# The last two up tiles of layer 0 by token halves, the context halves between the two halves of the last down product

## The chip, the cores and the metric

The kernel runs on one core of one Trainium2 chip. The metric is the device time of one execution in microseconds (us), the median of several runs; lower is better. Engine names are the profile's: PE multiplies matrices, DVE and POOL are the vector engines, ACT is the scalar engine, SP issues the transfers.

## The reference

A trunk of two layers works on 256 latent tokens and 256 context tokens of width 1024, in float32. Each layer is a token mixer of four branches and then a gated convolutional feed-forward network (FFN). Cut to the FFN and what follows it:

```python
def conv_ffn(h, w_up, conv_w, conv_b, w_down):          # D_FF = 2816
    a, g = jnp.split(h @ w_up, 2, axis=-1)
    return (jax.nn.silu(dwconv(a, conv_w, conv_b)) * g) @ w_down   # conv of 3 tokens

x = x + mod[:, 5] * rmsnorm(conv_ffn(h, ffn_up[l], ...), norm_g[l, 3])
...
h = rmsnorm(x, norm_g[l, 0]) * (1.0 + mod[:, 1]) + mod[:, 0]       # the next layer's input
```

Context tokens pass through layer 0 with the same weights and a modulation of their own; in layer 1 only the latent tokens go through the FFN, but both kinds are read by the mixer.

## The kernel before, in words

Activations lie with channels on the partitions and the 512 tokens along the free axis, latents in columns 0 to 255, context in 256 to 511. Each float32 product is made of three products of reduced-precision (`fp32r`) parts: `hi*hi`, `hi*lo`, `lo*hi` (`mm3`, lines 135 to 137), where `lo` is the value less its rounded `hi`. A weight tile of 128x1024 takes this way: SP loads it into one of 4 buffers `raw`, ACT rounds it into `hi` (L122), and DVE (one instruction) or POOL (four of 256 columns) subtracts to make `lo` (L131). `wload` deals the tiles out: `turn[1]` is the share of POOL, 0.6 in the FFN of layer 0 and 0.8 from its last down product on. There are 4 buffers of `hi` and 4 of `lo`, so the cast of a tile waits until PE is done with the tile loaded four before.

Layer 0's FFN has 22 tiles of 128 hidden channels. `up(i, ...)` multiplies tile i's two weight tiles with the normed input `h2` into two PSUM banks, `ua` (to be convolved) and `ug` (the gate); then ACT scales `ua` (L1482), DVE adds the two neighbours (L1486, L1488, after which the bank is free), ACT applies silu (L1490), DVE multiplies by `ug` (L1491), ACT rounds to `fh` (L1492) and POOL subtracts to `fl` (L1493). `ua`, `ug` and the down product's `o` share a PSUM pool (`mm`) of 3 banks. The hidden channels are taken in three segments, tiles 0 to 5, 6 to 13 and 14 to 21; after each, `out_gemm` multiplies the segment with the down weights and adds into `y`. The last segment's down product runs by token halves, 8 output tiles m for the latents, then 8 for the context; the second half goes through m backwards, and the weights of m = 4 to 7 are kept in their buffers from the first half (`keep`=4), so that 12 weight tiles are loaded for the 16 products.

After a half of the last segment, `chain` follows for it: a sum of squares over the output channels (PE row sums `st`, L170; DVE `rs_v`, L176; POOL `rs_y`, L151; PE spreads it into `R`, L182), the scaled addition into `x` channel tile by channel tile (DVE L341; POOL or DVE L343; ACT squares, L279; DVE adds them, L285), a second `st`, `rs_v`, `rs_y`, `R`, and the next layer's input `hn` (DVE L300, ACT L301, DVE L302). `chain` is a generator; `pump()` advances it one step, and `gemm_p` calls `pump` in the middle and at the end of each product of 24 matmuls. So its steps stand between matmuls by count: the latents' chain is pumped through the context's down product, the context's chain through the first products of layer 1 (Fourier `f`, then `u`). Tile's scheduler may move an instruction a little; each engine then executes its own queue in order. `hn` lies in the same buffers as `h2`.

## Time and profile before

| | us |
|---|---|
| median of 3 runs | 1406.83 (1405.43 to 1408.57) |
| the profiled execution, whole | 1407.98 |
| its span in the trace | 1406.2 |
| PE busy in the span | 1336.9 (95%) |
| DVE, ACT, POOL busy | 863.8, 621.6, 849.7 |

The span is what the trace shows from the first to the last instruction; the execution's own time lies 1.8 us above it. All starts below are counted from the span's start. Layer 0 ends and layer 1 begins at about 908 us.

### The profile page before, as it was taken

The page shows a single profiled execution, that of the slowest core. Times are in us where ns is not written, and L with a number is a line of the kernel's source. Part 1 is how long each engine was busy: PE and PEld are TensorE (multiplying, and loading weights), DVE is VectorE, ACT ScalarE, POOL GpSimd, SP SyncE. Part 2 cuts the span into 40 slices and gives each one's busy share as a digit, 9 for nine tenths or more (in the row PEclk, how much of TensorE's full clock was granted, in tenths as well). Part 3 has the DMA queues.
Part 4 walks back from the last instruction along what each step waited for, and adds up shares of the span by engine and source line. Part 5 has one row for each costly group of instructions (what it writes and reads, how often), then busy time and mean ns, then how long its engine had stood idle before and what let it go on. Part 6 is the DMA issues. An engine that isn't in the chain of part 4 may idle for free. (4 is left out here: it accounts for less than half of the span.)

```text
span 1406.2 us, 22765 instructions
## 1 busy us (share of the span) xinstructions
PE 1336.9 (95%) x8514; PEld 1195.1 (85%) x8514; DVE 863.8 (61%) x1554; ACT 621.6 (44%) x1098; POOL 849.7 (60%) x978
## 2 busy tenths in 40 slices
PE   8798999999999979999799999898999999899998
PEld 6597899888878979888688889897999998899997
DVE  4738766888777465599886553768847543532323
ACT  4435534444324445423231333466636545554443
POOL 1533234456764676567565546675556898689894
PEclk9999999999999999999899999999999999999999
DMA  9422223433443443466577443343324455355552
GB/s 347 137 77 81 69 105 106 135 120 140 160 162 107 147 151 114 138 227 211 195 253 270 155 160 106 116 135 104 108 76 135 147 164 184 123 184 200 183 181 75
DMA packets 61935, 210.55 MB, mean 150 GB/s; under 512 B 7145, under 2 KB 9729, under 8 KB 61569
## 3 DMA queue, kind: packets, MB, share of 16 engines
q1 hardware_dynamic: 61824, 209.10, 44.1%
q8 instruction: 67, 1.10, 0.3%
q14 instruction: 44, 0.35, 0.1%
HBM read 208.01 MB, written 1.06 MB: 149 GB/s over the span
## 5 line engine op out<-in xcount | busy, mean ns | idle before, releaser
L131 POOL TENSOR_TENSOR lo<-raw,hi 128x256 fp32r<-128x256 f32 x814 | 698.6, 890 | 392.2 <-ACT hi L122 373.9
L122 ACT CAST hi<-raw 128x1024 fp32r<-128x1024 f32 (+2 forms) x284 | 293.7, 1036 | 336.1 <-PE ua L136 76.6
L131 DVE TENSOR_TENSOR lo<-raw,hi 128x1024 fp32r<-128x1024 f32 (+2 forms) x79 | 122.3, 1548 | 89.6 <-ACT hi L122 89.5
L135 PE MATMUL gt<-hh,hi 128*128 128x512 f32 (+1 forms) x512 | 175.3, 342 | 1.0 <-DVE sig L782 1.0
L137 PE MATMUL gt<-hh,lo 128*128 128x512 f32 (+1 forms) x512 | 172.8, 338 | 0.6 <-POOL lo L131 0.6
L136 PE MATMUL gt<-hl,hi 128*128 128x512 f32 (+1 forms) x512 | 172.2, 336 | 0.0
L135 PE MATMUL ug<-hh,hi 128*128 128x256 f32 (+1 forms) x384 | 125.9, 328 | 10.4 <-DVE ca L1488 10.4
L232 DVE SCALAR_TENSOR_TENSOR ar<-ar,scb 128x1024 f32<-128x1024 f32 x80 | 122.4, 1534 | 15.6 <-DMA ar<-w_adaT 14.8
L136 PE MATMUL ug<-hl,hi 128*128 128x256 f32 (+1 forms) x384 | 125.5, 327 | 0.0
L135 PE MATMUL ua<-hh,hi 128*128 128x256 f32 (+1 forms) x384 | 124.3, 324 | 0.9 <-ACT hh L301 0.9
L137 PE MATMUL ug<-hh,lo 128*128 128x256 f32 (+1 forms) x384 | 125.1, 326 | 0.0
L136 PE MATMUL ua<-hl,hi 128*128 128x256 f32 (+1 forms) x384 | 124.0, 323 | 0.1
L137 PE MATMUL ua<-hh,lo 128*128 128x256 f32 (+1 forms) x384 | 123.8, 322 | 0.0
L137 PEld LDWEIGHTS gt<-hh,lo 128*128 128x128 f32 x512 | 96.6, 189 | 11.6 <-POOL lo L131 0.8
L135 PEld LDWEIGHTS gt<-hh,hi 128*128 128x128 f32 x512 | 96.7, 189 | 11.0 <-DVE sig L782 1.2
L136 PEld LDWEIGHTS gt<-hl,hi 128*128 128x128 f32 x512 | 96.8, 189 | 10.0
L135 PEld LDWEIGHTS ug<-hh,hi 128*128 128x128 f32 x384 | 74.2, 193 | 16.9 <-issue 8.5
L135 PE MATMUL o<-fh,hi 128*128 128x256 f32 (+1 forms) x240 | 81.0, 337 | 0.0
L136 PE MATMUL mm<-lo,hh 128*128 128x256 f32 x272 | 78.6, 289 | 2.4 <-DVE lo L131 2.4
L136 PE MATMUL o<-fl,hi 128*128 128x256 f32 (+1 forms) x240 | 80.5, 335 | 0.0
L137 PE MATMUL o<-fh,lo 128*128 128x256 f32 (+1 forms) x240 | 80.5, 335 | 0.0
L135 PEld LDWEIGHTS ua<-hh,hi 128*128 128x128 f32 x384 | 72.8, 190 | 7.6 <-ACT hh L301 1.1
(312 smaller groups left out, 3250.6 us busy)
## 6 DMA issues: line engine op xcount, KB each, us to landing
raw<-w_up SPq DMA_DIRECT2D x92, 512.0 KB, 4.0
ar<-w_adaT SPq DMA_DIRECT2D x80, 512.0 KB, 4.1
raw<-w_gate SPq DMA_DIRECT2D x64, 512.0 KB, 3.5
raw<-w_tm SPq DMA_DIRECT2D x24, 512.0 KB, 3.5
raw<-w_dr SPq DMA_DIRECT2D x22, 512.0 KB, 3.5
raw<-w_dn SPq DMA_DIRECT2D x20, 512.0 KB, 3.7
ada_w<-w_ada SPq DMA_DIRECT2D x16, 512.0 KB, 8.3
raw<-w_branch SPq DMA_DIRECT2D x16, 512.0 KB, 3.6
```

What stands on the lines that cost most here:

```text
L122: nc.scalar.copy(hi[:, :n], raw[:, :n])
L131: e.tensor_tensor(out=lo[:, s], in0=raw[:, s], in1=hi[:, s].bitcast(F32), op=ALU.subtract)
L135: nc.tensor.matmul(ps, a[0], b[0], start=start, stop=False)
L136: nc.tensor.matmul(ps, a[0], b[1], start=False, stop=False)
L137: return nc.tensor.matmul(ps, a[1], b[0], start=False, stop=stop)
L232: nc.vector.scalar_tensor_tensor(out=raw if st == ns - 1 else junk, in0=raw, scalar=0.5, in1=scb[:, st, :], op0=ALU.mult, op1=ALU.mult, ac ...
```

## The change

The up tiles 20 and 21 of layer 0 are computed by halves: before the last down product for the latents only, with their weights loaded, and again between the two halves of that product for the context, with the same four weight tiles loaded and split a second time. The last down product keeps no weights (`keep=0`), so its second half loads m = 0 to 7 again, in forward order. The output projection `w_out` still keeps four.

```diff
--- before.py
+++ after.py
@@ -1395,7 +1395,7 @@
                         nc.sync.dma_start(out=x[c0][k], in_=I["xT"][:, k, c0:c0 + 256])
             yn = None if last else YNorm(zap, TQ, "za")
 
-            def out_gemm(parts, act, src, yn, ks, w0=0, n=1024, add=False, stat=False, lag=0, nt=0):
+            def out_gemm(parts, act, src, yn, ks, w0=0, n=1024, add=False, stat=False, lag=0, nt=0, keep=CFG["keep"]):
                 kept = {}
                 late = []
                 for c0, c1 in parts:
@@ -1405,7 +1405,7 @@
                     for i, m in enumerate(ms):
 
                         wt = kept.pop(m, None) or wload(src(m), n)
-                        if c0 == 0 and len(parts) > 1 and m >= KD - CFG["keep"]:
+                        if c0 == 0 and len(parts) > 1 and m >= KD - keep:
                             kept[m] = wt
                         ps = mmb("o")
                         if c0 == 0 and i < lag:
@@ -1553,8 +1553,19 @@
                           nc.gpsimd if CFG["yp"] & 2 else None)
             yn = None if last else YNorm(zap, TQ, "za")
             for s, (a, b) in enumerate([] if last else SEGS):
-                ups(nu, min(b + 1, KF))
+                split = 2 if s == 2 else 0
+                ups(nu, min(b + 1, KF) - split)
                 nu = min(b + 1, KF)
+
+                def part_ups(c0, c1):
+                    for i in range(KF - split, KF):
+                        if c0 == 0:
+                            f[i] = new_f()
+                        w2 = [wload(I["w_up"][l, i, q]) for q in range(2)]
+                        up(i, w2[0], w2[1], c0, c1, f[i])
+
+                if split:
+                    part_ups(*parts[0])
                 nk = b - a
                 acts = [f[a + j] for j in range(nk)]
                 if s == 2:
@@ -1574,9 +1585,11 @@
                     if not last:
                         A1n = mod_scale(P[1]["vec"], mods[1], 1, 0, True)
                         hn.append(new_h())
-                    for c0, c1 in out_gemm(parts, acts, src, yn, range(nk), add=True, stat=True, lag=CFG["dl"]):
+                    for c0, c1 in out_gemm(parts, acts, src, yn, range(nk), add=True, stat=True, lag=CFG["dl"], keep=0):
                         pump(64)
                         pend.append(chain(yn, c0, c1, G2, hn[0], A1n, mods[1], 0, CFG["g3"][c0 > 0]))
+                        if c0 == 0:
+                            part_ups(*parts[1])
             tick(len(todo))
 
     es_ctx = ExitStack()
```

Three places of the instruction queues, with buffer numbers kept in the names. First POOL, at the end of the latents' down product, before: the first `rs_y` of the latents' chain stands behind the subtracts of the last down weights (`lo_8237` is m = 7).

```order
L131 TENSOR_TENSOR lo_8126<-raw_8123,hi_8125 128x256 x4
L131 TENSOR_TENSOR lo_8199<-raw_8196,hi_8198 128x256 x4
L131 TENSOR_TENSOR lo_8237<-raw_8234,hi_8236 128x256 x4
L151 TENSOR_TENSOR rs_y_8291<-rs_v_8289,mh_98 128x2
L131 TENSOR_TENSOR lo_8435<-raw_8432,hi_8434 128x256
L343 TENSOR_TENSOR x0_0_4494<-x0_0_4494,y0_5891 128x256
L131 TENSOR_TENSOR lo_8435<-raw_8432,hi_8434 128x256 x3
```

Behind it come the four context weights that this half has to load (`lo_8435` is the first).

POOL in the changed kernel at the same `rs_y`; `lo_8279`, `lo_8288` and `lo_8382` are weight tiles of the context's up halves (the fourth, `lo_8376`, is on DVE), `lo_8469` is the context's first down weight.

```order
L131 TENSOR_TENSOR lo_8237<-raw_8234,hi_8236 128x256 x4
L131 TENSOR_TENSOR lo_8279<-raw_8276,hi_8278 128x256 x4
L131 TENSOR_TENSOR lo_8288<-raw_8285,hi_8287 128x256 x4
L131 TENSOR_TENSOR lo_8382<-raw_8379,hi_8381 128x256 x4
L151 TENSOR_TENSOR rs_y_8310<-rs_v_8308,mh_98 128x2
L131 TENSOR_TENSOR lo_8469<-raw_8466,hi_8468 128x256
L343 TENSOR_TENSOR x0_0_4494<-x0_0_4494,y0_5891 128x256
L131 TENSOR_TENSOR lo_8469<-raw_8466,hi_8468 128x256 x3
```

The `rs_y` now stands behind the fourth up weight. Second, DVE in the changed kernel, in the latents' chain just before its second `st`; `ca_8458` is tile 21's context half.

```order
L343 TENSOR_TENSOR x0_5_4499<-x0_5_4499,y5_5896 128x256
L341 SCALAR_TENSOR_TENSOR y6_5897<-y6_5897,ms5_7955,R_8324 128x256
L341 SCALAR_TENSOR_TENSOR y7_5898<-y7_5898,ms5_7955,R_8324 128x256
L285 TENSOR_TENSOR sq_8329<-sq_8329,sq_8438 128x256
L1486 SCALAR_TENSOR_TENSOR ca_8458<-ua_8388,vec_100,ca_8458 128x255
L285 TENSOR_TENSOR sq_8329<-sq_8329,sq_8455 128x256
L1488 SCALAR_TENSOR_TENSOR ca_8458<-ua_8388,vec_100,ca_8458 128x255
L343 TENSOR_TENSOR x0_7_4501<-x0_7_4501,y7_5898 128x256
L131 TENSOR_TENSOR lo_8610<-raw_8607,hi_8609 128x1024
L1491 TENSOR_TENSOR ca_8458<-ca_8458,ug_8389 128x256
```

The additions that free the bank of `ua_8388` and the product with `ug_8389` now stand between the chain's additions of squares. PE's queue there, where `o_8475` and `o_8516` are the context's down products of m = 0 and 1, and `fh_7877` and `fl_7878` are tile 21:

```order
L135 MATMUL o_8516<-fh_7392,hi_8509 128x256
L136 MATMUL o_8516<-fl_7393,hi_8509 128x256
L135 MATMUL o_8475<-fh_7877,hi_8468 128x256
L137 MATMUL o_8516<-fh_7392,lo_8510 128x256
L135 MATMUL o_8516<-fh_7477,hi_8509 128x256
L136 MATMUL o_8475<-fl_7878,hi_8468 128x256
L137 MATMUL o_8475<-fh_7877,lo_8469 128x256
L136 MATMUL o_8516<-fl_7478,hi_8509 128x256
```

The second output tile is begun before the first ends, and the first waits for tile 21's context half. The second `st` of the latents' chain follows five rows below this; it and the second `R` have exactly as many matmuls behind the end of the latents' down product as before, 132 and 144. Third, POOL at the start of layer 1, before: the first `rs_y` of the context's chain, `lo_8904` the fifth weight tile of layer 1.

```order
L131 TENSOR_TENSOR lo_8663<-raw_8660,hi_8662 128x256 x4
L131 TENSOR_TENSOR lo_8807<-raw_8804,hi_8806 128x256 x4
L151 TENSOR_TENSOR rs_y_8683<-rs_v_8681,mh_98 128x2
L131 TENSOR_TENSOR lo_8904<-raw_8901,hi_8903 128x256 x4
L343 TENSOR_TENSOR x256_0_4513<-x256_0_4513,y0_5891 128x256
L343 TENSOR_TENSOR x256_2_4515<-x256_2_4515,y2_5893 128x256
L343 TENSOR_TENSOR x256_4_4517<-x256_4_4517,y4_5895 128x256
L131 TENSOR_TENSOR lo_8913<-raw_8910,hi_8912 128x256 x3
```

Ahead of this `rs_y` stand layer 1's second and third weight tiles.

And in the changed kernel, where `lo_8989` and `lo_9032` are layer 1's third and fourth weight tiles and `lo_9089` its fifth:

```order
L131 TENSOR_TENSOR lo_8845<-raw_8842,hi_8844 128x256 x4
L131 TENSOR_TENSOR lo_8989<-raw_8986,hi_8988 128x256 x4
L131 TENSOR_TENSOR lo_9032<-raw_9029,hi_9031 128x256 x4
L151 TENSOR_TENSOR rs_y_8865<-rs_v_8863,mh_98 128x2
L343 TENSOR_TENSOR x256_0_4513<-x256_0_4513,y0_5891 128x256
L131 TENSOR_TENSOR lo_9089<-raw_9086,hi_9088 128x256 x4
L343 TENSOR_TENSOR x256_2_4515<-x256_2_4515,y2_5893 128x256
L343 TENSOR_TENSOR x256_4_4517<-x256_4_4517,y4_5895 128x256
L343 TENSOR_TENSOR x256_6_4519<-x256_6_4519,y6_5897 128x256
```

The fourth tile was on DVE before and is on POOL now, ahead of `rs_y`; the fifth moved from ahead of `x256_0` to between `x256_0` and `x256_2`. On ACT the copy `ft` that the second Fourier product reads (L822) stood behind the square of `x256_0`, and stands behind that of `x256_2` now.

## Rows read from the trace of the kernel before

**Rows 1.** Timeline of PE, 842 to 920 us: start, duration, instruction, [idle before, releaser].

```profile
842.22 0.39 PE L135 MATMUL ua<-hh,hi 128*128 128x512 f32 x1
...
853.10 0.28 PE L135 MATMUL o<-fh,hi 128*128 128x256 f32 x1
...
875.50 0.50 PE L170 MATMUL st<-one,sq 128*128 128x1 f32 x4
...
879.20 0.61 PE L182 MATMUL R<-cst,rs_y 128*128 128x128 f32 x4
...
893.16 0.58 PE L170 MATMUL st<-one,sq 128*128 128x1 f32 x4 [0.75 <-DVE sq L285]
895.35 0.61 PE L170 MATMUL st<-one,sq 128*128 128x1 f32 x4 [1.61 <-ACT sq L279]
...
900.62 1.22 PE L182 MATMUL R<-cst,rs_y 128*128 128x128 f32 x4 [3.09 <-POOL rs_y L151]
...
908.37 0.50 PE L170 MATMUL st<-one,sq 128*128 128x1 f32 x4
...
919.15 0.48 PE L847 MATMUL f<-dft,ft 128*128 128x256 f32 x1 [2.01 <-ACT ft L822]
```

**Rows 2.** Table by stretch, two of 5 us; its first line names the columns.

```profile
core 0: us, PE busy (x) PEld busy (x) DVE busy (x) ACT busy (x) POOL busy (x), PEclk, DMA share, GB/s
...
895.00:900.00 5.00, 2.18 (x16) 1.92 (x16) 2.19 (x5) 2.92 (x5) 5.00 (x8) 0.73 0.61 210
900.00:905.00 5.00, 4.38 (x24) 4.38 (x25) 3.05 (x7) 1.08 (x3) 3.33 (x5) 0.59 0.43 132
```

**Rows 3.** Timeline of POOL, 859 to 901 us.

```profile
859.55 10.17 POOL L131 TENSOR_TENSOR lo<-raw,hi 128x256 fp32r<-128x256 f32 x12 [1.25 <-ACT hi L122]
...
893.53 6.37 POOL L131 TENSOR_TENSOR lo<-raw,hi 128x256 fp32r<-128x256 f32 x8 [1.80 <-ACT hi L122]
899.87 0.69 POOL L151 TENSOR_TENSOR rs_y<-rs_v,mh 128x2 f32<-128x2 f32 x1
```

**Rows 4.** Groups of DVE, 879.2 to 900.6 us: count | busy, mean ns | idle before, releaser.

```profile
L285 DVE TENSOR_TENSOR sq<-sq 128x256 f32<-128x256 f32 x10 | 6.6, 672 | 3.5 <-ACT sq L279 3.5
L341 DVE SCALAR_TENSOR_TENSOR y<-y,ms,R 128x256 f32<-128x256 f32 x8 | 3.5, 472 | 0.0
L317 DVE TENSOR_TENSOR y<-y,o 128x256 f32<-128x256 f32 x6 | 2.5, 412 | 1.9 <-PE o L137 1.9
```

**Rows 5.** Timeline of PE in layer 1, at the mLSTM's first product.

```profile
974.68 0.64 PE L1027 MATMUL pu<-cst,mlEM 36*128 36x36 f32 x4 [6.69 <-ACT mlEM L1020]
```

**Rows 6.** Groups of all engines, 853 to 909 us.

```profile
L131 POOL TENSOR_TENSOR lo<-raw,hi 128x256 fp32r<-128x256 f32 x39 | 31.1, 828 | 11.9 <-ACT hi L122 11.9
L135 PEld LDWEIGHTS o<-fh,hi 128*128 128x128 f32 x128 | 24.7, 193 | 0.0
...
L122 ACT CAST hi<-raw 128x1024 fp32r<-128x1024 f32 x13 | 13.6, 1044 | 11.7 <-PE o L136 7.6 <-POOL lo L131 2.0 <-PE ug L136 1.4
...
L151 POOL TENSOR_TENSOR rs_y<-rs_v,mh 128x2 f32<-128x2 f32 x2 | 1.4, 696 | 8.0 <-DVE rs_v L176 8.0
```

**Rows 7.** Timeline of PE, 515 to 538 us, where up tiles already run by halves.

```profile
515.63 0.71 PE L182 MATMUL R<-cst,rs_y 128*128 128x128 f32 x4 [0.21 <-POOL rs_y L151]
...
527.74 0.35 PE L135 MATMUL ug<-hh,hi 128*128 128x256 f32 x1 [2.42 <-DVE ca L1488]
...
537.66 0.71 PE L182 MATMUL R<-cst,rs_y 128*128 128x128 f32 x4
```

**Rows 8.** Timeline of POOL, 914 to 930 us.

```profile
914.31 3.18 POOL L131 TENSOR_TENSOR lo<-raw,hi 128x256 fp32r<-128x256 f32 x4 [0.47 <-ACT hi L122]
917.46 2.08 POOL L343 TENSOR_TENSOR x<-x,y 128x256 f32<-128x256 f32 x3
...
927.01 2.35 POOL L131 TENSOR_TENSOR lo<-raw,hi 128x256 fp32r<-128x256 f32 x4 [1.67 <-ACT hi L122]
```

**Rows 9.** Groups of POOL, 500 to 580 us: the subtract after an up half.

```profile
L1493 POOL TENSOR_TENSOR fl<-ca,fh 128x256 fp32r<-128x256 f32 x8 | 7.0, 880 | 8.8 <-ACT fh L1492 8.8
```

## The prediction

> **What bounds the kernel now.** I read the table by stretch over the whole span first. PE is busy nearly everywhere, so a change pays where PE idles or where its clock is down. Around the change that is one place, the second half of the last down product, and the timeline of PE shows what it waits for there. The latents' half ends at 875.50 with the first `st`; the latents' `R` follows at 879.20, and from then on PE multiplies the context's down product while the chain runs on DVE, ACT and POOL. At 893.16 and 895.35 PE stands for the second `st` (0.75 and 1.61 us), at 900.62 for the second `R` (3.09 us), 5.45 us in all; the product ends at 908.37 [rows 1]. With the waits the granted clock falls to 0.73 and 0.59 in two stretches of 5 us, so a part of each ran at the lower of the two levels, 1.2 GHz. PE was busy 2.18 and 4.38 us in them, which at the full clock would have been 0.27 x 2.18 + 0.41 x 4.38 = 2.4 us less [rows 2]. So 7.8 us are lost here at most.
>
> What is the chain's pace? From `R` to `R` it takes 900.62 - 879.20 = 21.4 us [rows 1]. PE has 120 matmuls of 256 columns between the two, 14.0 us at 0.1167 (below), and about 1 us of `st` and `R`. The chain is the longer by more than 6 us, and that is the wait. Its last piece is a queue: two weight tiles' subtracts hold POOL from 893.53 to 899.90, and `rs_y` comes right behind them [rows 3].
>
> The next loss behind it, 6.69 us at `pu` in layer 1, is a chain that starts from a product of layer 1 itself [rows 5]. It moves with PE and absorbs nothing.
>
> **The change part by part.** *The halves on PE.* A matmul of 512 columns costs (853.10 - 842.22)/48 = 0.2267 us, one of 256 costs (875.50 - 853.10)/192 = 0.1167 [rows 1]. Tiles 20 and 21 were 96 of the first kind, 21.76 us, and become 192 of the second, 22.40: **+0.64**. Their weight loads double as well; a load takes 0.193 [rows 6], more than the 0.1167 between matmuls, so it lies beside them in the half product already.
>
> *The weights loaded again.* Eight more tiles, four up and four down: eight transfers, eight casts of 1.04 us on ACT, and by the queues six sets of four subtracts on POOL (4 x 0.828 = 3.31 us each) and two on DVE [rows 6]. The transfers I cost at nothing, since the four `raw` buffers let each start a tile's work ahead. POOL is the engine to count: from the start of the latents' down product to the end of the context's it now has 16 of 20 tiles, 53.0 us, four `fl` of 0.88 [rows 9], four additions of 0.69 [rows 8] and two `rs_y` of 0.70 [rows 6], 60.7 us. PE needs 480 x 0.1167 = 56.0 us, and the `st` and `R` some 2.6 (what the half before leaves for them, 908.37 - 875.50 - 22.4 - 7.8 [rows 1]): 58.6 us without waits. So POOL is no cover for a PE that does not wait, but it is enough for one that does, and I cost it at nothing in the sum.
>
> *The first `rs_y`.* It stands behind the fourth up tile's subtracts now. Their cast needs the buffer of the last latent down weight, which is free at about 875.66; cast 1.04, subtracts 3.31, `rs_y` 0.70 give an `R` at 880.7 where it was 879.20: **+1.5**. With the quickest set in the trace, 2.35 [rows 8], it is +0.5, with the slow ones (10.17/3 = 3.39 [rows 3]) +1.6. Queued behind `rs_y` on POOL are the first context weight and `x0_0`, and the whole chain waits for that `R`.
>
> *The wait that the change goes for.* The extra 96 matmuls do not come between the two `R`. In PE's queue the second `st` and `R` follow the latents' product after 132 and 144 matmuls before and after, because the chain is pumped by matmul groups; the up tiles are pumped in place of down tiles. So the chain's own length decides. Out of it go the context's takes and part of its squares (6 x 0.412 and about half of 10 x 0.672, 5.8 us of DVE); into it come six operations of two up tiles (2.8 us at 0.472) [rows 4]. If DVE alone set the pace that would be -3.0. But the trace has the very mixture: from 515.63 to 537.66 a chain runs beside up halves, `R` to `R` in 22.0 us, and PE waits 2.42 us for a PSUM bank that DVE L1488 frees late [rows 7]. In the changed queues the same L1488 of tile 21 stands between the chain's squares, and `o_8516` needs its bank; then `o_8475` needs `fh_7877`, queued behind as well. So the waits for `st` and `R` turn into waits for a bank and for tile 21. Bounds -3.0 and +0.6; I take **0**, nearest to the rows of the same mixture. The clock then falls as before: **0**, with -2.4 if it stays up.
>
> *The start of layer 1.* Before, the Fourier product at 919.15 came 10.8 us after the end of the down product at 908.37 [rows 1]. Now, counted from that end: the fourth tile's cast can begin at 0.2, its subtracts at 1.2 or when the third's are done (its buffer is free 2.8 us earlier, so 1.7), hence `rs_y` at 5.0, `R` at 5.7, the scaled product at 6.3 to 6.8 (`R` takes 0.61 [rows 1], L341 0.47 [rows 4]), `x256_0` to 7.5, the fifth tile's four subtracts to 10.8, and then `x256_2`. Before, `x256_0` began at 917.46 [rows 8], 1.7 us ahead of the Fourier product, and `ft` now waits for `x256_2` in that manner: 12.5, or +1.7. With subtracts of 2.35 it is -0.7; if POOL is a little behind from the five tiles that it does in the 16.8 us after the `R`, up to +3.0. I take **+1.3**, between them.
>
> Sum: 0.64 + 1.5 + 0 + 0 + 1.3 = +3.4 us. The profiled execution took 1407.98 and would take 1411.4; it lies 1.15 above the median of the runs, 1406.83, which makes **1410.2** there. A measurement of this kernel can tell 0.2%, 2.8 us, from no change: below 1404.0 is faster, above 1409.6 slower.
>
> **The rivals.** *The wait is filled (faster).* If the chain takes at most 15 us from `R` to `R`, the waits and the dip go: -7.8 + 0.64 = -7.2. POOL then takes back 60.7 - 58.6 = 2.1, so about -5.1, or 1401.7. It begins to pay once the chain is under 18 us. For it: DVE has less to do. Against it: the 22.0 us of [rows 7].
>
> *POOL too late with the weights (slower).* If POOL idles beside its 60.7 us as it did for 11.9 us behind casts [rows 6], it becomes the bound once that idling passes some 5 us, since PE with its 1.5 and some 6 us of waits takes about 66; 9 us of it would add 4 to the sum: 1414.2. Against it: most of that idling came where four kept tiles left nothing to load.
>
> *Layer 1 decides.* Eight tiles more shift which later tile falls to DVE and which to POOL, and the queues of layer 1 differ in many places. I cannot price it but by the size of a wait there, part of 6.69 [rows 5]: 4 us either way about 1407.5, the chain's terms cancelling.
>
> *Loads that don't overlap.* If a load of 128 columns into the whole array had to wait for the matmul before it, 96 loads more at 0.193 would give +18.5 and 1425. The half product contradicts this: 192 loads and 192 matmuls in 22.40 us. The Trainium skill (TensorE: Matmul & The Clock Gate, The mechanism) says that a load overlaps running matmuls only when it goes to other row groups of the array, and every load here takes all rows; by it this rival would hold, and the trace does not agree.
>
> **How the numbers follow.** The forecast, the wait moved and two more before and behind it, gets 0.55; it spans 0 to +6 us, most of it above 2.8 (slower 0.38, same 0.16, faster 0.01). The filled wait gets 0.17 (faster 0.14, same 0.03), late weights 0.12 (slower 0.11, same 0.01), layer 1 0.15 (faster 0.04, same 0.06, slower 0.05), loads 0.01. That makes faster 0.19, same 0.26, slower 0.55. The range from 1402.5 to 1414.5 reaches to about the middle of the filled wait and of the late weights, and leaves out under 0.1 on each side; the forecast's own is 1406.8 to 1412.8.
>
> **What would show it.** In the changed profile, PE's first `R` after the latents' product should show a wait of 1 to 1.5 us for `rs_y`; then waits for DVE L1488 and for `fh` or `fl` in the first two context tiles, 5 to 7 us with some at `st`, a clock below 0.9 in the 5 us that follow, and 21 to 22 us from `R` to `R`. In the rest of the context's half PE should not wait for `lo`. The Fourier product should start 11 to 13 us after the down product's end. A chain under 18 us, or a clock that stays at 1.00, would make the sum wrong on the fast side; waits of PE for `lo` on the slow side.

## The result, and the profile after

The changed kernel takes 1420.8 us (median of 4 runs, 1419.6 to 1421.8), the kernel before on the same chip 1406.7: a ratio of 1.0099, with a 95% interval of 1.0081 to 1.0116. The direction was forecast, the size was not: the prediction had 1410.2 and a range to 1414.5. The profiled execution has a span of 1419.6 us against 1406.2, 13.4 more.

To see where the 13.4 us lie, one puts the same events of both timelines side by side. The common start is the first `ua` of tile 20, the last moment at which both programs are alike. In the kernel before:

```profile
831.34 0.39 PE L135 MATMUL ua<-hh,hi 128*128 128x512 f32 x1
```

The timeline of PE in the changed kernel; all waits of over 0.3 us between 865 and 940 us are among them, then `pu` and two rows of layer 1:

```profile
831.16 0.28 PE L135 MATMUL ua<-hh,hi 128*128 128x256 f32 x1
...
865.92 0.58 PE L170 MATMUL st<-one,sq 128*128 128x1 f32 x4 [0.47 <-DVE sq L285]
...
870.07 0.71 PE L182 MATMUL R<-cst,rs_y 128*128 128x128 f32 x4 [0.16 <-POOL rs_y L151]
...
873.49 0.28 PE L135 MATMUL ua<-hh,hi 128*128 128x256 f32 x1
...
876.37 0.28 PE L135 MATMUL ug<-hh,hi 128*128 128x256 f32 x1
...
882.71 0.39 PE L136 MATMUL o<-fl,hi 128*128 128x256 f32 x1 [0.70 <-POOL fl L1493]
885.71 0.36 PE L135 MATMUL o<-fh,hi 128*128 128x256 f32 x1 [2.50 <-ACT hi L122]
888.54 0.58 PE L135 MATMUL o<-fh,hi 128*128 128x256 f32 x1 [2.00 <-ACT fh L1492]
891.01 1.70 PE L170 MATMUL st<-one,sq 128*128 128x1 f32 x8
895.28 1.05 PE L182 MATMUL R<-cst,rs_y 128*128 128x128 f32 x4
...
914.83 0.58 PE L170 MATMUL st<-one,sq 128*128 128x1 f32 x4 [1.06 <-DVE sq L285]
...
920.82 0.93 PE L182 MATMUL R<-cst,rs_y 128*128 128x128 f32 x4 [2.02 <-POOL rs_y L151]
928.08 1.99 PE L847 MATMUL f<-dft,ft 128*128 128x256 f32 x8 [1.44 <-ACT ft L822]
...
982.74 0.64 PE L1027 MATMUL pu<-cst,mlEM 36*128 36x36 f32 x4 [6.71 <-ACT mlEM L1020]
...
1058.71 0.38 PE L135 MATMUL yb<-bh,hi 128*128 128x256 f32 x1 [1.39 <-ACT sig L778]
...
1065.42 0.39 PE L135 MATMUL gt<-hh,hi 128*128 128x256 f32 x1 [0.58 <-DVE za L782]
```

Against [rows 1, 5] the stretches come out as follows.

| stretch | before | after | difference |
|---|---|---|---|
| span's start to first `ua` of tile 20 | 831.34 | 831.16 | -0.2 |
| that `ua` to the latents' first `R` | 47.86 | 38.91 | -8.95 |
| first `R` to second `R` | 21.42 | 25.21 | +3.8 |
| second `R` to the first `st` at the product's end | 7.75 | 19.55 | +11.8 |
| that `st` to the Fourier product (L847) | 10.78 | 13.25 | +2.5 |
| Fourier product to `pu` | 55.53 | 54.66 | -0.9 |
| `pu` to the end of the span | 431.52 | 436.86 | +5.3 |

The second and the fourth line hold the work that was moved. One half costs (876.37 - 873.49)/24 = 0.120 us a matmul, so 48 matmuls of 0.2267 (10.9 us) became 96 of 0.120 (11.5) ahead of the first `R` and 96 more behind it: 21.8 - 11.5 = 10.3 us less in the second line are the move, and that `R` is 1.3 us late. In the fourth line 96 down matmuls, 11.2 us, now stand behind the second `R` and not ahead of it; 0.6 us are left. So the loss is about 8 us around the boundary, and 5.3 in layer 1, behind a `pu` whose own wait has not changed (6.69 and 6.71).

At the boundary the waits are where the prediction put them: 0.70, 2.50 and 2.00 us in the first context tiles, 5.2 in all, where the kernel before had 5.45 at `st` and `R`. What differs is the clock behind them. The table by stretch of the changed kernel (the columns in its first line; PEclk is the granted clock):

```profile
core 0: us, PE busy (x) PEld busy (x) DVE busy (x) ACT busy (x) POOL busy (x), PEclk, DMA share, GB/s
880.00:885.00 5.00, 2.42 (x17) 1.82 (x15) 3.01 (x7) 3.19 (x7) 4.18 (x7) 1.00 0.33 105
885.00:890.00 5.00, 2.28 (x11) 2.02 (x12) 3.05 (x5) 1.86 (x5) 2.37 (x3) 0.70 0.38 119
890.00:895.00 5.00, 5.00 (x25) 5.00 (x25) 0.58 (x2) 1.33 (x2) 2.02 (x3) 0.50 0.27 91
895.00:900.00 5.00, 5.00 (x36) 5.00 (x35) 3.98 (x7) 2.27 (x4) 4.66 (x7) 0.77 0.30 105
```

Worked out as for [rows 2], the lower level costs 0.30 x 2.28 + 0.50 x 5.00 + 0.23 x 5.00 = 4.3 us here, against 2.4 before. A row of 5 us mixes both levels, so one cuts the table where the level changes: first the changed kernel, then the kernel before.

```profile
887.03:888.54 1.51, 0.00 (x0) 0.00 (x0) 1.02 (x2) 0.40 (x1) 0.00 (x0) 0.50 0.55 138
888.54:895.28 6.74, 6.74 (x31) 6.64 (x32) 0.58 (x2) 1.36 (x2) 3.02 (x5) 0.50 0.36 125
895.28:897.27 1.99, 1.99 (x11) 1.99 (x11) 1.25 (x4) 1.68 (x3) 1.98 (x4) 0.50 0.00 0
```
```profile
897.53:900.62 3.09, 0.00 (x2) 0.00 (x1) 0.42 (x1) 1.23 (x2) 3.09 (x6) 0.50 0.51 170
900.62:904.08 3.46, 3.46 (x16) 3.46 (x17) 2.13 (x5) 0.91 (x2) 2.71 (x4) 0.50 0.46 152
```

PE was busy 8.73 us at the lower level in the changed kernel, and before 3.46 us and 0.28 just ahead of the wait; by half of that the fall costs some 4.4 us against 1.9. Before, nearly half of the low stretch lay in the wait for the second `R`, where it is free; here only 1.51 us of it did.

Why are those tiles late? The timeline of POOL, of ACT and of DVE in the changed kernel, in this order:

```profile
872.39 2.50 POOL L131 TENSOR_TENSOR lo<-raw,hi 128x256 fp32r<-128x256 f32 x3
874.85 0.74 POOL L343 TENSOR_TENSOR x<-x,y 128x256 f32<-128x256 f32 x1
877.11 3.01 POOL L131 TENSOR_TENSOR lo<-raw,hi 128x256 fp32r<-128x256 f32 x4 [1.52 <-issue]
880.08 0.74 POOL L343 TENSOR_TENSOR x<-x,y 128x256 f32<-128x256 f32 x1
```

```profile
880.85 0.42 ACT L279 ACTIVATE sq<-x 128x256 f32<-128x256 f32 x1 [3.25 <-POOL x L343]
...
882.74 0.54 ACT L1482 ACTIVATE ca<-ua,vec 128x256 f32<-128x256 f32 x1
...
888.09 0.40 ACT L1492 CAST fh<-ca 128x256 fp32r<-128x256 f32 x1 [1.59 <-DVE ca L1491]
```

```profile
885.10 0.47 DVE L1488 SCALAR_TENSOR_TENSOR ca<-ua,vec,ca 128x255 f32<-128x255 f32 x1
```

Tile 21's `ua` is done by 876.7, but ACT begins its `ca` at 882.74: ACT stands 3.25 us for the square of an `x` whose addition POOL does behind a weight tile's four subtracts. So L1488, which frees the bank, ends at 885.57, and `fh` at 888.49. The row of 885.71 is put down to ACT `hi`; that tile's own cast, the second behind the halves, began at 875.95, and the bank came free 0.14 us before the row.

### The profile page after: what moved, and what is told of

Its sections match the earlier page's. It is cut to its first block, busy times and chain, and to the rows that moved or that the text cites. A ratio compares the mean times of both kernels' runs of the same rounds, so it can differ in the third digit from the quotient of the medians.

```text
span 1419.6 us, 23040 instructions
## 1 busy us (share of the span) xinstructions
PE 1346.6 (95%) x8610; PEld 1206.6 (85%) x8610; DVE 867.9 (61%) x1562; ACT 631.2 (44%) x1112; POOL 870.6 (61%) x1003
## 5 line engine op out<-in xcount | busy, mean ns | idle before, releaser
L131 POOL TENSOR_TENSOR lo<-raw,hi 128x256 fp32r<-128x256 f32 x837 | 715.7, 888 | 379.7 <-ACT hi L122 354.8
L122 ACT CAST hi<-raw 128x1024 fp32r<-128x1024 f32 (+2 forms) x292 | 302.1, 1036 | 334.6 <-PE ua L136 70.9
L131 DVE TENSOR_TENSOR lo<-raw,hi 128x1024 fp32r<-128x1024 f32 (+1 forms) x81 | 123.7, 1527 | 89.5 <-ACT hi L122 89.5
L135 PE MATMUL ua<-hh,hi 128*128 128x256 f32 (+1 forms) x400 | 127.4, 319 | 0.9 <-ACT hh L301 0.9
L137 PE MATMUL ug<-hh,lo 128*128 128x256 f32 (+1 forms) x400 | 128.1, 320 | 0.0
L136 PE MATMUL ua<-hl,hi 128*128 128x256 f32 (+1 forms) x400 | 127.0, 317 | 0.1
L137 PE MATMUL ua<-hh,lo 128*128 128x256 f32 (+1 forms) x400 | 126.8, 317 | 0.0
L135 PEld LDWEIGHTS ug<-hh,hi 128*128 128x128 f32 x400 | 77.3, 193 | 16.4 <-issue 8.6
L1493 POOL TENSOR_TENSOR fl<-ca,fh 128x256 fp32r<-128x256 f32 (+1 forms) x50 | 54.3, 1086 | 45.6 <-ACT fh L1492 45.6
L135 PEld LDWEIGHTS ua<-hh,hi 128*128 128x128 f32 x400 | 76.2, 190 | 7.0 <-ACT hh L301 1.1
```

What stands on the lines that cost most here:

```text
L122: nc.scalar.copy(hi[:, :n], raw[:, :n])
L131: e.tensor_tensor(out=lo[:, s], in0=raw[:, s], in1=hi[:, s].bitcast(F32), op=ALU.subtract)
L135: nc.tensor.matmul(ps, a[0], b[0], start=start, stop=False)
L136: nc.tensor.matmul(ps, a[0], b[1], start=False, stop=False)
L137: return nc.tensor.matmul(ps, a[1], b[0], start=False, stop=stop)
L1493: nc.gpsimd.tensor_tensor(out=f[1][:, c0:c1], in0=a[:, :n], in1=f[0][:, c0:c1].bitcast(F32), op=ALU.subtract)
```

## The experiments

Two theories were set against each other in each run. Theory 1: the loss has two independent halves, the place of the context halves beside the latents' chain, and the deal of weight tiles in layer 1. All ratios are to the kernel before, in runs on the same chip, with 95% intervals; the labels name the kernels from here on.

**Layer 1: only the deal.** e0 is the kernel before with this at the end of its last down product (e19 is the same without the second line), e1 the changed kernel with the reverse:

```diff
+                    turn[0] = round((turn[0] + 0.4) % 1.0, 6)
+                    wn[0] += 8
```
```diff
+                    turn[0] = round((turn[0] + 0.6) % 1.0, 6)
+                    wn[0] -= 8
```

> The kernel before, with the count that deals weight tiles to DVE and POOL moved on by eight tiles at the end of layer 0's last down product; layer 0 is untouched. Theory 1 (in layer 1 the change loses only because eight more tiles shift that deal): 1411 to 1415 us, +5.3 from the pu wait to the end as in the changed kernel, with the waits for ACT sig and DVE za near 1059 to 1071 there again, and 0 to +2.5 about the start of layer 1. Theory 2 (the deal is of no account, layer 1 loses because of what the boundary leaves behind): 1406.7 within 1 us.

> The changed kernel, with the deal of weight tiles set back at the end of layer 0's last down product, so that layer 1's tiles go to the engines to which they went before the change. Theory 1: 1412.5 to 1415.5 us; the 8 us about the boundary stay, the 5.3 in layer 1 go. Theory 2: 1420.8 within 1.5 us.

> As e0, but only the count that deals the subtracts to DVE and POOL is moved on; the count that picks the buffers of the weight tiles is left. Theory 1 (which engine subtracts which tile is what costs layer 1): as e0, 0.3 to 0.5% above before. Rival (it is the buffers that the tiles fall into): within 0.15% of before.

e0: 1.0039 (1.0025 to 1.0053). e19: 1.0043 (1.0031 to 1.0055). e1: 1.0048 (1.0034 to 1.0063), about half of the changed kernel's 1.0099. The waits of layer 1 come with the deal alone; the timeline of PE in e0:

```profile
1050.30 0.39 PE L135 MATMUL yb<-bh,hi 128*128 128x256 f32 x1 [1.38 <-ACT sig L778]
...
1058.50 0.39 PE L135 MATMUL gt<-hh,hi 128*128 128x256 f32 x1 [0.58 <-DVE za L782]
```

The reader is to see the 1.39 and 0.58 us of the changed kernel again, in a program whose layer 0 is that of before. In e1 they are gone, and `pu` to the end takes 431.26 us, as before (431.52). So the loss in layer 1 belongs to eight tiles more in a round robin: by the medians 5.5 us between e0 and the kernel before, and some 7 between the changed kernel and e1, the start of layer 1 included. By its median e19 says that the counter that picks the engine is enough. Its one profile does not show how: the wait of 1.39 us is not there, and `pu` to the end takes 434.4 us, 2.9 more than before, where e0 has 438.8. Which waits make up the rest of the loss is open. In e1 the loss at the boundary stays: from tile 20's first `ua` to `pu` 150.70 us, where the kernel before has 143.34.

**Where the context halves stand.** e2 computes both halves of tiles 20 and 21 ahead of the down product, with the weights loaded twice; e3 is the kernel before, which loads four down tiles twice; e20 leaves the products in the changed order and starts the chain behind the halves. All with the deal set back.

```diff
 e2                 if split:
                        part_ups(*parts[0])
+                       part_ups(*parts[1])
```
```diff
 e3  -out_gemm(parts, acts, src, yn, range(nk), add=True, stat=True, lag=CFG["dl"])
     +out_gemm(parts, acts, src, yn, range(nk), add=True, stat=True, lag=CFG["dl"], keep=0)
```
```diff
 e20 -                   pend.append(chain(yn, c0, c1, G2, ...))
                         if c0 == 0:
                             part_ups(*parts[1])
     +                   pend.append(chain(yn, c0, c1, G2, ...))
```

> Both halves of tiles 20 and 21 ahead of the down product, latents' then context's, with the weights loaded twice as in the change; nothing stands between the halves of the down product, whose four last weights are kept as before, and the deal is set back. Theory 1 (the boundary loses because the context halves stand between the two halves of the down product, in the latents' chain's way): 1406.5 to 1409 us, the 0.64 of the narrower matmuls and little more. Rival (halves and second loads cost the time wherever they stand): 1412 or more.

> The kernel before, in whose last down product of layer 0 no weight is kept from the latents' half to the context's: four down tiles are loaded, cast and subtracted again, nothing else; the deal is set back behind it. Theory 1 (POOL's work on reloaded weights is not what costs the 8 us, the place of the context halves is): within 2 us of before, 1405 to 1409. Rival (late weights on POOL): 1410.5 or more, with PE waiting for lo in the context's half.

> The changed kernel with the deal set back (as e1), and the latents' chain of this boundary started behind the context halves, not ahead of them: the order of the products on PE is that of the change, but the chain's R, additions and squares now run beside down tiles alone, as before the change. Theory 1 (the loss is that the halves' evictions and the chain stand in one another's way): the waits for L1488 and fh of tile 21 go, R to R 20 to 22 us with the waits for st and R of before, and the time 0 to 0.2% above before. Rival (split, second loads and POOL's subtracts cost it wherever the chain runs): 0.35% or more above before.

e2: 1.0009 (1.0000 to 1.0018), and its `R` to `R` is 21.43 us, that of before. e3: 0.9996 (0.9985 to 1.0007). So neither the second loads nor the split as such costs what e1 loses. e20: 1.0029 (1.0018 to 1.0041), more than theory 1 had. Its `R` to `R` of 21.91 us with 5.45 us of waits at `st` and `R` is as expected, but the first `R` stands 51.15 us behind tile 20's `ua`, 3.3 more than before: the halves take 1.3 of that by the step above, and waits of 0.47 for the first `st` and of 0.83 for `fl` in the first context tile come to it; 0.7 us stay open. That last wait is the one of the next group: it comes also where no chain runs beside the halves.

e12 splits tile 21 alone, and was to show half of the loss.

```diff
-                split = 2 if s == 2 else 0
+                split = 1 if s == 2 else 0
```

> The changed kernel with only tile 21 in halves (24 matmuls of 512 columns fewer are split, one context half between the halves of the down product, not two), the deal set back behind it. Theory 1 (each context half between the two R puts its evictions and its weights' subtracts into the chain's way): the loss falls by more than half of e1's 0.48%, to 0.1 to 0.25% above before, because the one half has the first context tiles' time behind it. Rival (the loss is a fixed price of reloading the weights and of the split's edges): 0.4% or more.

It is worse than e1: 1.0074 (1.0060 to 1.0088); theory 1 in this form falls. Its timeline of PE:

```profile
886.27 0.58 PE L135 MATMUL o<-fh,hi 128*128 128x256 f32 x1 [4.95 <-ACT fh L1492]
```

One context half gives the wait of two, 4.95 us for 5.2: that fits a price of the last tile, which the first down tile needs at once, and not a price per half. Why it is worse than e1 is not shown. Its Fourier product comes 15.24 us behind the end of the product (12.81 in e1), with a wait of 2.93 us at the context's first `st` (1.56 in e1); the second `R` falls 11.9 us ahead of that end, and e4 and e8 below, with the same 11.9, are late there too.

**What tile 21 waits for.** e7 and e15 take work off POOL: the latents' chain adds `x` on DVE, or the context halves' four up tiles are subtracted there. e4 and e8 leave more matmuls between the two `R`.

```diff
 e7   -            e = nc.gpsimd if k < CFG["paddk"] and k % 2 == 0 else nc.vector
      +            e = nc.gpsimd if k < pk and k % 2 == 0 else nc.vector     # pk = 0 for this chain
 e15  -                        w2 = [wload(I["w_up"][l, i, q]) for q in range(2)]
      +                        w2 = [wload(I["w_up"][l, i, q], dve=c0 > 0) for q in range(2)]
 e4   -        for _ in range(CFG["ys"][3]):
      +        for _ in range(CFG["ys"][3] + w3):     # w3 = 4 for this chain
 e8   = e4 and e7
```

> The changed kernel with the deal set back (as e1), and the latents' chain of this boundary adds x on DVE in all eight rows, where POOL took every second. Theory 1 (ACT's ca of tile 21 is late because ACT stands for squares of x0_2 and x0_4, whose additions stand on POOL behind weight subtracts): the waits for L1488 and fh of tile 21 go or fall below 1 us each, R to R comes to 21 to 22 us from 25.2, and the time to 3 to 5 us less than e1, 0.1 to 0.3% above before. Rival (DVE is what is late, with two tiles' ca, fl and takes among the chain's work): DVE gets four more additions, the waits stay or grow, and the time is that of e1 or more.

> The changed kernel with the deal set back (as e1), and the four weight tiles of the context halves subtracted on DVE, where POOL took three of them. Theory 1 (POOL's subtracts delay the first rs_y by 1.5 us and the additions of x on which ACT's queue stands): the first R 1 to 1.5 us earlier than e1's (37.4 to 37.9 after the first ua of tile 20, where e1 has 38.9), the waits for L1488 and fh of tile 21 together below 3 us instead of 4.5, and the time 2 to 4 us less than e1, 0.2 to 0.35% above before. Rival (DVE is what is late): the waits grow, time of e1 or more.

> The changed kernel with the deal set back (as e1), and in the latents' chain of this boundary four empty steps ahead of the second st, so that PE meets that st after 180 matmuls of the context's share and the R after 192, not after 132 and 144. Theory 1 (what PE waits for there is the PSUM bank that ca of tile 21 frees and fh of tile 21, and not st and R): no gain on e1, 0.48% above before within 0.2%; the waits of 2.5 and 2.0 us for L1488 and fh stay. Rival (the chain is too long for the matmuls set between the two R, as the prediction reasoned): 3 to 4 us less than e1, some 0.2% above before, the clock back at 1.00 from 890 on.

> Both edits, e4 and e7. Theory 1: the tile's waits go with the additions, and the waits for st and R that might take their place go with the later place; 5 to 7 us less than e1, at or just below before. Rival (DVE late): the time of e1 or more.

e7: 1.0043 (1.0029 to 1.0057). Its timeline of PE:

```profile
884.70 0.51 PE L135 MATMUL o<-fh,hi 128*128 128x256 f32 x2 [3.22 <-ACT fh L1492]
886.32 0.58 PE L136 MATMUL o<-fl,hi 128*128 128x256 f32 x1 [1.00 <-POOL fl L1493]
...
891.64 0.61 PE L182 MATMUL R<-cst,rs_y 128*128 128x128 f32 x4
```

The wait for the bank has gone and `R` to `R` falls from 25.21 to 21.99, as expected; but those for `fh` and `fl` have grown to 4.2 us, as the rival has it, and the time is above the 0.1 to 0.3% of theory 1. Up to `pu` the profile has 3.9 us less than e1 (146.82 for 150.70), but the median shows no gain outside the intervals. In this execution `pu` to the end took 2.7 us more, with the same program there (the last section); whether that holds for the median is not shown. e15: 1.0051 (1.0039 to 1.0064), no gain where theory 1 had 2 to 4 us; its first `R` comes 0.9 us earlier than e1's, so that wait was POOL's, but the additions then stand behind the down tiles' subtracts, and the waits for L1488 and `fh` stay (2.53 and 1.42). e4: 1.0074 (1.0058 to 1.0090); e8: 1.0063 (1.0047 to 1.0079). Both miss: e4 is worse than e1 and not level with it, and e8 is far from the 5 to 7 us that theory 1 gave it. More room for the chain is no help: the waits of 2.50 and 2.00 stay in e4, its `R` to `R` becomes 31.5 us, and the Fourier product comes 2.4 us later behind the product's end than in e1. The rival that the chain is too long for its matmuls falls.

**The first context tiles.** In the latents' half the last eighth of two down tiles, the only one that needs tile 21, is put off; in the context's half it is not. e25 does that in e1 alone, e21 in e7; e24 and e26 are e21 with one and two weight tiles of the Fourier product on DVE; e23 is e20 with the edits of e7 and e24.

```diff
+                        if c0 and i < lagc:          # lagc = 2 here
+                            gemm(ps[:, :c1 - c0], wt, act, c0, c1, ks=ks[:4], last=False)
+                            pump()
+                            gemm(ps[:, :c1 - c0], wt, act, c0, c1, ks=ks[4:-1], w0=4, first=False, last=False)
+                            pump()
+                            late.append((m, wt, ps, i))
+                            if i < lagc - 1:
+                                continue
```
```diff
 e24 -wt = [wload(I["w_tm"][l, 4, kh]) for kh in range(2)]
     +wt = [wload(I["w_tm"][l, 4, kh], dve=kh == 0) for kh in range(2)]
```

> The changed kernel with the deal set back (as e1) and the last eighth of the first two context down tiles put off as in e21; the additions stay on POOL. Theory 1 (two causes in a row: tile 21's eviction is late because ACT's queue stands for the additions on POOL, and PE needs it at once): about half of what e21 gained on e1, 0.25 to 0.45% above before, with 1.5 to 3 us left of the waits for fh and fl. Rival (the place of the last eighth alone is the cause, the additions do nothing): e21's 0.19% or less.

> e7 (deal set back, additions on DVE) with the last eighth of the first two context down tiles, the only one that needs tile 21, put off until both tiles' other seven stand, as the latents' half does it. Theory 1 (the first context tiles wait for tile 21's eviction, which runs late among the chain's operations): the waits for fh and fl, 4.2 us in e7, fall by 1.5 to 2.5 us, and the time to 0.2 to 0.35% above before. Rival (a wait moved is a wait kept, since the chain is late by as much): the waits come back at st and R, and the time is e7's.

> e21 with the first weight tile of layer 1's Fourier product subtracted on DVE. Theory 1 (in e21 29 subtracts stand on POOL without a break from 887 to 910 and the context chain's rs_y behind them; that wait of 2.97 us is the larger part of what e21 still loses at the end of the context's product): the wait falls below 1 us, and the time to 0.15% below to 0.1% above before. Rival (DVE becomes late by as much): e21's 0.19% above before or more.

> As e24, with both weight tiles of layer 1's Fourier product on DVE. Theory 1: no more than e24 gains, since rs_v is then the last to come: within 0.1% of e24. Rival (POOL is late all through the start of layer 1, each tile less helps): 0.15% or more below e24.

> e20 with the chain's additions of x on DVE and the first weight tile of layer 1's Fourier product subtracted on DVE, the two edits of e16. Theory 1 (split and chain apart, the split itself costs 0.64 us, and the two edits give what they gave the kernel before, 0.1%): from 0.1% below to 0.1% above before. Rival (the second loads cost more once nothing else is late): 0.3% or more above before.

e25: 1.0033 (1.0021 to 1.0045); e21: 1.0019 (1.0006 to 1.0031); e24: 0.9999 (0.9987 to 1.0011); e26: 1.0008 (0.9993 to 1.0022); e23: 1.0009 (0.9997 to 1.0020). Four of the times lie where theory 1 put them, and e21's just below its 0.2 to 0.35%. Of e7 and e25, which make one edit each, neither is clear of e1 by its interval; e21, which makes both, is. `R` to `R` is 25.21 us in e1, 21.08 in e25, 21.99 in e7 and 17.33 in e21; in e25 and e21 114 matmuls stand between the two `R` and not 120, which is 0.7 us of it. The timeline of PE, the table by stretch and the timeline of POOL in e21 (its line 1496 is L1488):

```profile
881.18 0.36 PE L135 MATMUL o<-fh,hi 128*128 128x256 f32 x1 [1.82 <-DVE ca L1496]
...
910.81 0.71 PE L182 MATMUL R<-cst,rs_y 128*128 128x128 f32 x4 [2.97 <-POOL rs_y L151]
```
```profile
880.00:885.00 5.00, 3.72 (x30) 3.55 (x31) 3.71 (x9) 2.42 (x5) 2.21 (x2) 1.00 0.42 121
885.00:890.00 5.00, 5.00 (x43) 5.00 (x44) 4.07 (x9) 4.10 (x8) 2.97 (x4) 1.00 0.24 88
```
```profile
887.03 23.07 POOL L131 TENSOR_TENSOR lo<-raw,hi 128x256 fp32r<-128x256 f32 x28 [2.22 <-ACT hi L122]
910.06 0.69 POOL L151 TENSOR_TENSOR rs_y<-rs_v,mh 128x2 f32<-128x2 f32 x1
```

With one wait of 1.82 us left, named by its true releaser, the clock stays at 1.00. What is won there comes back in part at the end: 28 subtracts (not 29) stand on POOL without a break, and the context chain's `R` waits 2.97 us behind them. In e24 that wait is 0.24, and the stretch from tile 20 to `pu` is 142.85 us, for 143.34 before and 150.70 in e1.

**The kernel before with the same edits.** e9 is the kernel before with e7's edit, e16 with e24's as well.

> The kernel before, with the latents' chain of this boundary adding x on DVE in all eight rows; up tiles whole as before. It tells whether what e7 gives belongs to the split. Theory 1 (before, that chain is held by POOL only at its last rs_y, 5.45 us of waits at st and R): R to R shorter by 0 to 2 us, time within 0.2% of before. Rival (the additions on POOL cost the kernel before as much as the changed one): 3 us or more below before.

> The kernel before with the additions of x on DVE (as e9) and one weight tile, the first of layer 1's Fourier product, subtracted on DVE, so that no subtract stands on POOL between rs_v and the chain's second rs_y. Theory 1 (before, that rs_y is the last thing that holds the R): the wait for rs_y, 1.40 us in e9, goes, R to R comes to 18.5 to 19.5 us, and the time to 0.1 to 0.3% below before. Rival (DVE's queue is late instead, the tile's subtract delays rs_v): R to R of 19.9 or more and the time of e9 or of before.

e9: 0.9989 (0.9977 to 1.0001), `R` to `R` 19.88 us. e16: 0.9988 (0.9980 to 0.9997). e16 is the only kernel here whose whole interval is below the kernel before, by 0.1%; the split at its best (e24) only comes level with before. The second `R` of e16 no longer waits, as theory 1 has it, but `R` to `R` is 20.36 us, longer than e9's and outside the 18.5 to 19.5 of theory 1, and the gain over e9 is none that shows. The `st` ahead of it is no later than in e9 (15.57 us behind the first `R` in both, after a wait of 2.37 and 2.35). What differs is the clock from that `st` to the `R`, in e16 and then in e9:

```profile
894.18:898.97 4.79, 4.79 (x23) 4.79 (x24) 2.88 (x6) 1.93 (x4) 1.14 (x2) 0.51 0.66 224
```
```profile
893.45:897.76 4.31, 2.91 (x20) 2.62 (x20) 2.36 (x5) 2.92 (x5) 3.44 (x6) 0.72 0.64 224
```

In e16 PE works through the whole stretch at the lower level, so that the `rs_v` that comes 1.7 us later behind the subtract on DVE, the rival's reading, is not even waited for.

## Why the prediction was right and wrong

**The halves, +0.64.** Mis-sized: 0.120 us a matmul makes 192 x 0.120 - 21.76 = +1.3. The price was taken from the down product, whose 192 matmuls come at 0.1167.

**The weights loaded again, 0.** Right within what can be told for the four down tiles: e3 is level, its interval ending 1 us above before. For the four up tiles e2, level within 0.2%, says the same.

**The first `rs_y`, +1.5.** Right in its size, 1.3, but not by the path that was reasoned. `rs_y` does stand behind the subtracts, and yet the `R` waits 0.16 us for it, where a wait of 1 to 1.5 was to be the sign. The `st` ahead of it is late already and waits 0.47 us for the last square; DVE and then POOL in the changed kernel:

```profile
864.82 0.96 DVE L285 TENSOR_TENSOR sq<-sq 128x256 f32<-128x256 f32 x1
```
```profile
866.54 2.82 POOL L131 TENSOR_TENSOR lo<-raw,hi 128x256 fp32r<-128x256 f32 x4 [0.17 <-ACT hi L122]
869.31 0.70 POOL L151 TENSOR_TENSOR rs_y<-rs_v,mh 128x2 f32<-128x2 f32 x1
```

That addition of squares takes 0.43 us before, and 0.42 in e15, where POOL is idle beside it; there `R` comes 0.9 us earlier. In e3, which loads no up tile again, the first `R` is 1.1 us late too, so the size is in part luck.

**The wait that the change goes for, 0, and the clock, 0.** This is the first step that failed. That the waits move from `st` and `R` to the bank of L1488 and to tile 21 was right, with 5.2 us for the 5 to 7 foretold. That the stretch would stay at 21 to 22 us was wrong: 25.2. The prediction read its 22.0 from [rows 7], where the same mixture runs, but there no down tile stands behind the last half that needs it at once. The fall of the clock was taken over from before, with what it cost there; but here it meets a PE that has work all through it. That the eviction of tile 21, put off among the chain's operations, is the cause is shown by e7 and e25, each of which takes one of the two reasons away (3.2 and 4.1 us of `R` to `R`), and by e21, which takes both (7.9); 0.7 us of e25's and of e21's are the six matmuls fewer. Of the 3.8 us the clock makes half of 6.74 - 0.28 us of PE's work at the lower level, 3.2; the halves' slower matmuls make 72 x 0.0033 = 0.2, the waits -0.2; some 0.5 us are not accounted for by rows.

**The start of layer 1, +1.3.** Right in its sign, 2.5 in its size; the Fourier product starts 13.25 us behind the product's end by the prediction's count, which had 11 to 13. Counted from the end of the product's last matmul it comes 10.62 us later in the kernel before, 14.31 in the changed one and 12.81 with the deal set back; so 1.5 of 3.7 us by that count are the deal again (2.1 in e0), which is what the prediction reasoned from. The other 2.2 stay in e1 and are gone in e2, e3 and e20: they come with the context halves beside the chain. 1.0 of them is more wait at the context's first `st` and 0.7 more at `ft`; why is not shown.

**Layer 1, 0.** This is the second step that failed, and the dearest: +5.3 us in the profiles. The prediction had it as a rival of 4 us either way, and as one that excludes the others; it came on top of the forecast. e0 and e1 show by their medians that the shift of the deal is enough to make all of it; the 5.3 itself is the difference of two single profiles, whose ends vary by more than 2 us (the last section).

**The rivals.** *The wait is filled* is what e21 makes of the change, 17.33 us with the clock at 1.00, and behind the product's end 1.8 us of it go again (14.61 us to the Fourier product, 12.81 in e1), where that rival's sum had 2.1 for POOL. *POOL too late with the weights* shows there only, at the very end. *Loads that don't overlap* did not show: 24 full loads and matmuls in 2.88 us in the context halves too. The section of the Trainium skill that the prediction cites there (TensorE: Matmul & The Clock Gate, The mechanism) also names a load into the background weight buffer as one that is pulled ahead of running matmuls, so by that section the rival need not hold.

## What to carry to other kernels

A split that moves work into a wait is to be costed from what stands directly behind its last piece on PE, and from how long the piece's eviction takes in the queues of ACT and DVE as they are there; counting the work between two ends of a chain misses it. Where weight tiles are dealt to engines by a running count, every tile more re-deals all that follows: set the count back when a local change is judged (it was worth some 5 of 13.4 us here), and try the deal as a change by itself. A fall of the clock is priced by PE's busy time in it, so a wait ahead of dense work costs more than the same wait ahead of other waits.

## What the runs showed of the hardware that was not expected

**DVE is slower beside POOL.** In the kernel before, DVE's L302 on tiles of one shape, and POOL at the same time:

```profile
903.53 0.87 DVE L302 SCALAR_TENSOR_TENSOR hl<-t,mod,hh 128x256 fp32r<-128x256 f32 x2
907.72 1.83 DVE L302 SCALAR_TENSOR_TENSOR hl<-t,mod,hh 128x256 fp32r<-128x256 f32 x2
```
```profile
901.91 1.42 POOL L131 TENSOR_TENSOR lo<-raw,hi 128x256 fp32r<-128x256 f32 x2
906.78 3.38 POOL L131 TENSOR_TENSOR lo<-raw,hi 128x256 fp32r<-128x256 f32 x4 [3.45 <-ACT hi L122]
```

The first two ran while POOL was idle (471 and 473 ns), the other two beside its subtracts (952 and 955). Of the 24 L302 of this chain in the traces of before, e1 and e12, the eight with nothing beside them on POOL took 468 to 478 ns, and of the sixteen beside a subtract fifteen took 944 to 964 and one 648. So the weight tiles on POOL also lengthen a chain that runs on DVE.

**The same layer 1 differs by 2 to 5 us from profile to profile.** Of the kernels whose layer 1 has the deal of before (but for a tile or two at its start), the profiles of before, e1, e15, e21 and e25 take 431.0 to 432.1 us from `pu` to the end, twelve others 433.8 to 435.9. In ten of these an operation on 128x1 elements on DVE, L1248, once took 2.55 to 2.59 us, which in the first five never took over 0.71. In e7, DVE and POOL:

```profile
1114.94 2.57 DVE L1248 TENSOR_TENSOR sm<-sm,neglam 128x1 f32<-128x1 f32 x1
```
```profile
1111.88 5.61 POOL L131 TENSOR_TENSOR lo<-raw,hi 128x256 fp32r<-128x256 f32 x8
```

and in e1, DVE at the same place:

```profile
1119.74 0.46 DVE L1248 TENSOR_TENSOR sm<-sm,neglam 128x1 f32<-128x1 f32 x1
```

DVE's operation in e7 ends at 1117.51, as POOL's run of eight subtracts does (1117.49). The Trainium skill (SBUF — State Buffer, SBUF: two separate sides) says that DVE and GpSimd share one pair of ports, for which a DVE instruction with two inputs in SBUF contends, and that whichever has it holds it for its whole instruction while the other is blocked. The rows agree that one blocks the other. The operation in e7 waits through more than one instruction, though: 2.57 us is more than three of POOL's subtracts of 0.70. No run here isolates the two engines. Each kernel was profiled once, so whether the long L1248 belongs to a kernel or to an execution is open, and the other two of the twelve (e20, e24) are long without it. For reading experiments it means that the end of one profile is uncertain by more than 2 us, and that a difference under 0.2% is read from the stretch that was edited and from the medians, not from a single span.
